# Earlier sums of squares and other unsplit half units in the second SSD layer of a four-layer encoder

## The chip, the cores and the metric

The kernel runs on one core of a Trainium2 chip. The metric is the device time of one execution in microseconds (us). Before the change it is 1605.35 us, the median of three runs (1604.55 to 1608.08). The profile is that of one further execution, which took 1607.9 us.

## The reference

The program is an encoder of four layers over 256 rows of width 1024, all in float32. Each layer is a mixer and an MLP, each behind an RMS norm and with a residual. Layers 0 and 3 have the SSD mixer, which the change is about; layer 1 has a dilated attention and layer 2 a differential attention.

```
def rmsnorm(x, g):
    xf = x.astype(jnp.float32)
    y = xf * lax.rsqrt(jnp.mean(xf * xf, axis=-1, keepdims=True) + RMS_EPS)
    return (y * g.astype(jnp.float32)).astype(x.dtype)
...
def ssd_mixer(h, in_w, conv_w, conv_b, dt_bias, a_log, d_skip, norm_g, out_w):
...
    zxbcdt = h @ in_w
    z, xbc, dt = jnp.split(zxbcdt, [SSD_D_INNER, SSD_D_INNER + SSD_CONV_CH], axis=-1)
...
    xbc = jax.nn.silu(xbc + conv_b)
    xs, bs, cs = jnp.split(xbc, [SSD_D_INNER, SSD_D_INNER + G * N], axis=-1)
...
    y_fwd = ssd_chunk_scan(xs, dt[:, :, 0], a[0], bs, cs)
    y_bwd = flip(ssd_chunk_scan(flip(xs), flip(dt[:, :, 1]), a[1], flip(bs), flip(cs)))
    y = y_fwd + y_bwd + d_skip.astype(jnp.float32).reshape(G, R)[..., None] * xs.astype(jnp.float32)
    y = y.reshape(bsz, s, SSD_D_INNER) * jax.nn.silu(z.astype(jnp.float32))
    y = rmsnorm(y, norm_g).astype(h.dtype)
    return y @ out_w
...
    for i in range(DEPTH):
...
        x = x + h
        x = x + sqrelu_mlp(rmsnorm(x, norm_mlp_g[i]), mlp_w1[i], mlp_w2[i])
    return rmsnorm(x, final_norm_g)
```

The in-projection `h @ in_w` has 6208 columns: 2048 for z, 2048 for x, 1024 for B, 1024 for C and 64 for dt.

## The kernel before, in words

**Layout and arithmetic.** The residual stream lies transposed in SBUF as eight tiles `xT` of 128 features by 256 rows. A float32 matrix product is made from fp32r matmuls: a weight tile is split into `whi` (ScalarE, a cast, line 117) and `wlo` (VectorE, raw minus whi, line 119), the activations likewise into a high and a low tile, and three matmuls (lines 150 to 152) add whi*high, whi*low and wlo*high. A half unit named in `native` skips the split: its raw weights are multiplied with whole float32 activations (line 148), so it needs neither line 117 nor line 119, and its raw buffer stays in use until its matmuls are done.

**Weights.** All weight chunks of a part are listed in the order of use. `pump` (called by `take` and `done`) issues their loads on the SyncE queue (`_dma`, line 105) into five `raw` buffers and their splits into five `whi` and five `wlo` buffers, four chunks ahead of the matmuls in this layer.

**The norm at the start of a layer.** While the MLP before it ends, each of the eight `xT` tiles is finished on VectorE (line 1179), split without its row factor (lines 234 and 235, tiles `spl`), and squared on ScalarE (line 243). GpSimd adds the squares of tiles 1 to 6 to that of tile 0, in the accumulator `sqacc` (line 245); tile 7 keeps its own. `norm_rows` then multiplies both with a constant matrix on TensorE (line 277, four matmul records), which sums over the features and leaves the sum in all partitions; ScalarE adds epsilon (line 279), and seven short VectorE operations (lines 259 to 264) give the reciprocal root `rbc`. `behind`, called on line 277, pins these matmuls behind the TensorE instruction written just ahead of them; later ones aren't held back by it.

**The SSD layer's order.** `ssd_events` lists the work as units with due times, and sorts them. A unit is 256 columns of the in-projection, in two halves of 512 input features; a half has four k tiles and two column tiles, so 24 split matmuls. For layer 3 the order is `CFG["order"]`: z0 z1 B0 x0 C0 x1 B1 x2 z2 C1 x3 C2 B2 z3 x4 and so on. The first two units and the dt unit (64 columns, due at 0.5) work on the unnormalised `spl` tiles and are multiplied by `rbc` when they leave PSUM ("defer"). After unit z0 come the row sums, the evacuation of z0, and `normalised`, which makes the eight tiles `nf` (line 304), `nh` (line 305) and `nl` (line 306) that all later units read; a native half reads `nf`. The dt tile is normalised on VectorE (line 507), transposed on TensorE (line 514, due at 1.5), and run through softplus and logarithm. The dt sums (line 548, due at 4.0) go to DRAM and come back as broadcast rows `bc` (line 579), to which VectorE adds a mask (line 582) and which ScalarE exponentiates (line 607); with `cb` (lines 589 and 591) this gives the factors G (line 620) of the output matmuls (line 632). The x, B and C units leave PSUM through a convolution on VectorE (line 488), and the PSUM banks of units alternate between two.

**The scheduler.** Within each engine the framework orders the instructions when the program is built, by priority (the order in which they are written) among those that its model takes as ready. So the order in a trace need not be that of the source.

Layer 0 has its own settings in `CFG0`, which override those of `CFG`; layer 3 uses `CFG` alone.

Of the kernel before, what the change touches and what calls it, by code (L numbers as in the profile page):

```python
# [51 lines left out]
class Prog:  # L52
# [360 lines left out]
    def ssd_events(self, l, finish):  # L413

        cfg = {**CFG, **(CFG0 if l == 0 else {})}
# [21 lines left out]
        def unit(kind, c0, defer):  # L437

            keys = [(l, kind, c0, i) + (("f32",) if f"{kind}{(c0 - base[kind]) // 256}.{i}" in cfg["native"] else ()) for i in range(2)]

            def fn(c0=c0):
                b = self.bank(f"r{st.setdefault('rot', 0) % 2}")
                st["rot"] += 1
                first = kind == "z" and c0 == 0
                xh, xl = (self.uh, self.ul) if defer else ([st["n"][0][:, k, :] for k in range(KD)], [st["n"][1][:, k, :] for k in range(KD)])
                for i in range(2):
                    wh, wl = self.take(keys[i])
                    for kk in range(4):
                        k = 4 * i + kk
                        for n in range(2):  # L450
                            c = slice(kk * 256 + n * P, kk * 256 + (n + 1) * P)
                            o = b[:, n * T:(n + 1) * T]
                            if wl is None:
                                self.mm3(o, wh[:, c], None, self.nf[:, k, :], None, k == 0 and n == 0, k == 7)
                            else:
                                self.mm3(o, wh[:, c], wl[:, c], xh[k], xl[k], k == 0 and n == 0, k == 7)
                    self.done()
                if first:
                    self.norm_rows("a0")
                evac(kind, c0, b.rearrange("p (n t) -> p n t", n=2), defer)  # L460
                if first:
                    st["n"] = self.normalised(gvec("g_mix", 8 * l, 8))
            plan = [(keys[i], in_w[i * 512:(i + 1) * 512, c0:c0 + 256].rearrange("(k p) f -> p k f", p=P)) for i in range(2)]
            return fn, plan
# [222 lines left out]
        for u, name in enumerate(cfg["order"].split()):  # L687
            kind, i = name[0], int(name[1:])
# [477 lines left out]
    def prepare_part(self, i):  # L1166
# [29 lines left out]
        for _, _, keys, _ in sorted(ev, key=lambda e: e[:2]):  # L1196
# [4 lines left out]

VEC, CST, HEAD = {}, {}, {}
CFG = dict(order='z0 z1 B0 x0 C0 x1 B1 x2 z2 C1 x3 C2 B2 z3 x4 z4 x5 x6 B3 C3 z5 x7 z6 z7',
           native=('B0.0', 'B0.1', 'x0.1', 'x1.1', 'x2.1', 'x3.1', 'x4.1', 'x5.1'),
           sums=4.0, rate=2.4, lag=1.3, tr=1.2, gh0=1.5, gh=0.8, y=2.95, olag=2.0, ogap=4.0, ntail=1, late=10, dt=0.5, defer=2, r2=0.25,
           n_th=1, n_yf=3, n_z2=4, n_bc=2, n_cb=1, n_xt=1, n_e=2, n_G=2, n_t1=1, n_sqt=1, n_ft=3, n_cvx=4, n_cvB=2, n_cvC=2)

CFG0 = dict(order='z0 z1 x0 C0 B0 x1 B1 x2 z2 C1 B2 x3 C2 x4 z3 z4 x5 C3 z5 B3 x6 x7 z6 z7',
            native=('x0.0', 'x0.1', 'B1.0', 'x1.1', 'x2.1', 'x3.1', 'z3.0', 'z4.0'),
            sums=4.75, rate=2.4, lag=1.3, tr=0.8, gh0=0.9, gh=0.4, y=3.2, olag=2.75, ogap=4.0, late=12, r2=0.05, dt=0.5,  # L1210
            n_z2=5, n_e=2, n_G=2, n_cvx=3, n_bc=2, n_cb=1, n_t1=1, n_xt=1, n_th=2, n_yf=1, n_cvB=2, n_cvC=1, n_ft=3)
DIL = dict(bias=2.5, v=5.5, vstep=0.75, s=9.4, sstep=3.7, tr=4.4, hstep=1.3, pv=4.7, out=74.8, ostep=2.2)
# [87 lines left out]
```

## Time and profile before

| what | before |
|---|---|
| median of the runs | 1605.35 us |
| the profiled execution | 1607.9 us |
| its span | 1606.1 us |
| TensorE busy | 1566.8 us (98%) |
| VectorE busy | 1203.5 us (75%) |
| ScalarE busy | 960.3 us (60%) |
| GpSimd busy | 134.1 us (8%) |
| layer 3's SSD mixer | from 1174.6 us to about 1417 us of the span |

PE is TensorE, PEld its weight loads, DVE VectorE, ACT ScalarE, POOL GpSimd, SP SyncE. A line of the timeline gives the start and the duration in us, the engine, the line of the kernel, the operation, what it writes and reads, how many instructions are merged, and in brackets the idle time of the engine before it with what ended it. Matmuls overlap, and their ends are modelled. PEclk is the share of the full TensorE clock that was granted.

### The profile page before, as it was taken

The numbers are of one execution on the slowest core, as the hardware profiler recorded it, in microseconds if no ns is written. First come the engines' busy times: TensorE is split into PE (matmuls) and PEld (weight loads), VectorE is DVE, ScalarE is ACT, GpSimd is POOL, SyncE is SP. The second block draws the span as 40 slices with busy tenths as digits, with TensorE's granted clock in tenths as the row PEclk, the third lists the DMA queues.
The fourth block names the chain that finished last, engine by engine and source line by source line (L and its number), as shares of the span: only waits on it lengthen the run. The fifth ranks groups of instructions, "written<-read, shape, count | busy, mean of one in ns | idle before, by whom it ended". The sixth has DMA issues, their size and how long they took to land.

```text
span 1606.1 us, 32218 instructions
## 1 busy us (share of the span) xinstructions
PE 1566.8 (98%) x12942; PEld 1519.4 (95%) x12942; DVE 1203.5 (75%) x1970; ACT 960.3 (60%) x1620; POOL 134.1 (8%) x120
## 2 busy tenths in 40 slices
PE   9999999999999999999999999999998999999998
PEld 8889899999999999999999999999988988899997
DVE  6999998455697777766556898655588999995554
ACT  6586865444667666655445777444455767664444
POOL 0012121000300000010000101000011122310001
PEclk9999999999999999999999999999999999999999
DMA  7677755676566555546666764666655767656661
GB/s 230 195 223 236 213 188 181 204 223 191 159 200 178 151 170 162 171 148 190 191 196 187 198 193 122 205 192 193 189 163 155 217 210 216 210 173 195 192 193 64
DMA packets 230293, 299.83 MB, mean 187 GB/s; under 512 B 16496, under 2 KB 166256, under 8 KB 230144
## 3 DMA queue, kind: packets, MB, share of 16 engines
q1 hardware_dynamic: 209552, 262.51, 53.4%
q10 hardware_dynamic: 20592, 35.27, 8.0%
q8 instruction: 101, 1.65, 0.4%
q14 instruction: 48, 0.39, 0.1%
HBM read 296.41 MB, written 3.62 MB: 187 GB/s over the span
## 4 chain that ended last, share of the span: by engine, by line
PE 73%; DVE 14%; DMA 5%; ACT 4%; issue 3%; POOL 1%; ACTq 0%; SPq 0%; DVEq 0%; POOLq 0%
PE r L151 12%; PE r L150 12%; PE r L152 12%; PE a L150 8%; PE a L152 8%; PE a L151 8%; DVE wlo L119 3%; DMA raw<-in_ssd_in_w_dram 2%; DMA bc<-scr 2%; PE r L148 2%; DVE cvx L488 1%; PE a L857 1%; PE a L858 1%; PE a L856 1%; DVE bc L582 1%
## 5 line engine op out<-in xcount | busy, mean ns | idle before, releaser
L119 DVE TENSOR_TENSOR wlo<-raw,whi 128x1024 fp32r<-128x1024 f32 (+1 forms) x490 | 592.8, 1217 | 291.4 <-ACT whi L117 287.9
L117 ACT CAST whi<-raw 128x1024 fp32r<-128x1024 f32 (+1 forms) x490 | 503.4, 1034 | 436.3 <-PE r L151 223.6
L151 PE MATMUL r<-spl,whi 128*128 128x256 f32 x1696 | 472.9, 279 | 4.7 <-DVE spl L235 4.7
L150 PE MATMUL r<-spl,whi 128*128 128x256 f32 x1696 | 475.1, 280 | 0.1
L152 PE MATMUL r<-spl,wlo 128*128 128x256 f32 x1696 | 471.4, 278 | 0.4 <-DVE wlo L119 0.4
L151 PEld LDWEIGHTS r<-spl,whi 128*128 128x128 f32 x1696 | 318.4, 188 | 6.5 <-DVE spl L235 6.1
L152 PEld LDWEIGHTS r<-spl,wlo 128*128 128x128 f32 x1696 | 318.6, 188 | 0.7 <-DVE wlo L119 0.6
L150 PEld LDWEIGHTS r<-spl,whi 128*128 128x128 f32 x1696 | 318.2, 188 | 0.6 <-DVE xT L1179 0.3
L150 PE MATMUL a<-hh,whi 128*128 128x256 f32 x944 | 261.4, 277 | 0.0
L151 PE MATMUL a<-hl,whi 128*128 128x256 f32 x944 | 261.3, 277 | 0.0
L152 PE MATMUL a<-hh,wlo 128*128 128x256 f32 x944 | 260.9, 277 | 0.0
L151 PEld LDWEIGHTS a<-hl,whi 128*128 128x128 f32 x944 | 177.6, 188 | 0.0
L150 PEld LDWEIGHTS a<-hh,whi 128*128 128x128 f32 x944 | 177.3, 188 | 0.2 <-ACT whi L117 0.2
L152 PEld LDWEIGHTS a<-hh,wlo 128*128 128x128 f32 x944 | 177.2, 188 | 0.0
L150 PE MATMUL r<-nh,whi 128*128 128x256 f32 x576 | 166.5, 289 | 7.3 <-DVE cvx L488 4.1
L152 PE MATMUL r<-nh,wlo 128*128 128x256 f32 x576 | 163.1, 283 | 1.9 <-DVE wlo L119 1.8
L151 PE MATMUL r<-nl,whi 128*128 128x256 f32 x576 | 162.2, 282 | 0.0
L245 POOL TENSOR_TENSOR sqacc<-sqacc,sq 128x256 f32<-128x256 f32 x48 | 44.5, 927 | 1090.7 <-ACT sq L243 1089.1
L150 PEld LDWEIGHTS r<-nh,whi 128*128 128x128 f32 x576 | 110.4, 192 | 11.8 <-issue 4.2
L152 PEld LDWEIGHTS r<-nh,wlo 128*128 128x128 f32 x576 | 110.1, 191 | 3.2 <-DVE wlo L119 2.3
L151 PEld LDWEIGHTS r<-nl,whi 128*128 128x128 f32 x576 | 109.9, 191 | 0.7 <-issue 0.4
L607 ACT ACTIVATE e<-bc,tb 128x256 f32<-128x256 f32 (+1 forms) x256 | 95.7, 447 | 6.1 <-DVE bc L582 4.8
(246 smaller groups left out, 2521.4 us busy)
## 6 DMA issues: line engine op xcount, KB each, us to landing
raw<-in_mlp_w_dram SPq DMA_DIRECT2D x256, 512.0 KB
raw<-in_ssd_in_w_dram SPq DMA_DIRECT2D x96, 512.0 KB
bc<-scr ACTq DMA_DIRECT2D x32, 768.0 KB
raw<-in_dil_qkv_w_dram SPq DMA_DIRECT2D x48, 512.0 KB
raw<-in_ssd_out_w_dram SPq DMA_DIRECT2D x32, 512.0 KB
raw<-in_dil_qkv_w_dram SPq DMA_DIRECT2D x64, 192.0 KB
raw<-in_diff_qkv_w_dram SPq DMA_DIRECT2D x24, 512.0 KB
raw<-in_dil_out_w_dram SPq DMA_DIRECT2D x8, 512.0 KB
```

The lines of the kernel that those rows point to most:

```text
L117: self.nc.scalar.copy(out=hi[:, :n], in_=raw[:, :n])
L119: self.nc.vector.tensor_tensor(out=lo[:, :n], in0=raw[:, :n], in1=hi[:, :n].bitcast(F32), op=ALU.subtract)
L148: mm(out, lhsT=wh, rhs=xh, start=start, stop=stop, skip_group_check=True)
L150: mm(out, lhsT=wh, rhs=xh, start=start, stop=False, skip_group_check=True)
L151: mm(out, lhsT=wh, rhs=xl, start=False, stop=False, skip_group_check=True)
L152: mm(out, lhsT=wl, rhs=xh, start=False, stop=stop, skip_group_check=True)
L245: nc.gpsimd.tensor_tensor(out=self.sqs[0], in0=self.sqs[0], in1=sq, op=ALU.add)
L488: nc.vector.scalar_tensor_tensor(out=u[:, n, lo:hi], in0=b[:, n, lo + d:hi + d], scalar=col("conv_w", w, cc), in1=u[:, n, lo:hi], op0=ALU. ...
L582: nc.vector.tensor_tensor(out=o, in0=o, in1=mask, op=ALU.add)
L607: X = lambda o, i_, bias: nc.scalar.activation(out=o, in_=i_, func=AF.Exp, bias=bias)
L856: mm(o, lhsT=self.uh[k][:, t], rhs=w_h, start=k == 0, stop=False)
L857: mm(o, lhsT=self.uh[k][:, t], rhs=w_l, start=False, stop=False)
```

## The change

Two edits. In `unit`, the call of `norm_rows` moves into the loop over the two halves and runs after the half that `cfg["rows"]` names: 0 in layer 3, which is after the first half of z0, and 1 in layer 0, which is where it stood. In `CFG`, the native half units change: both halves of B0 become split, and the first half of B1 and the first half of z3 become native. Their number stays eight.

```
                             else:
                                 self.mm3(o, wh[:, c], wl[:, c], xh[k], xl[k], k == 0 and n == 0, k == 7)
                     self.done()
-                if first:
-                    self.norm_rows("a0")
+                    if first and i == cfg["rows"]:
+                        self.norm_rows("a0")
                 evac(kind, c0, b.rearrange("p (n t) -> p n t", n=2), defer)
...
 CFG = dict(order='z0 z1 B0 x0 C0 x1 B1 x2 z2 C1 x3 C2 B2 z3 x4 z4 x5 x6 B3 C3 z5 x7 z6 z7',
-           native=('B0.0', 'B0.1', 'x0.1', 'x1.1', 'x2.1', 'x3.1', 'x4.1', 'x5.1'),
+           native=('B1.0', 'x0.1', 'x1.1', 'x2.1', 'x3.1', 'x4.1', 'x5.1', 'z3.0'), rows=0,
...
-            native=('x0.0', 'x0.1', 'B1.0', 'x1.1', 'x2.1', 'x3.1', 'z3.0', 'z4.0'),
+            native=('x0.0', 'x0.1', 'B1.0', 'x1.1', 'x2.1', 'x3.1', 'z3.0', 'z4.0'), rows=1,
```

## The prediction

> **What bounds the kernel now.** I read the page first (span, chain), then the table of what TensorE waited for in the second SSD layer (1168 to 1412 us of the span), then the busy time by stretch at the places of those waits, then the timelines of the engines around the start of that layer. From the page:
>
> ```profile
> span 1606.1 us, 32218 instructions
> ...
> PE 73%; DVE 14%; DMA 5%; ACT 4%; issue 3%; POOL 1%; ACTq 0%; SPq 0%; DVEq 0%; POOLq 0%
> ```
>
> The chain that ended last runs on TensorE for 73% of the span, so a change pays only where it takes work or waiting off TensorE. The waits of TensorE in this layer, in the columns total us, times, longest:
>
> ```profile
> PE r L632 <- DVE G L620: 2.8, 2, 2.4
> PE r L589 <- ACT xt L601: 2.7, 1, 2.7
> PE r L589 <- DVE cvC L491: 2.4, 1, 2.4
> PE r L150 <- DVE cvx L488: 2.3, 1, 2.3
> PE r L632 <- DVE t L638: 1.9, 1, 1.9
> PE r L514 <- DVE dtT L507: 1.7, 1, 1.7
> PE r L151 <- DVE spl L235: 0.4, 1, 0.4
> ```
>
> These seven rows sum to 14.2 us. Two of them lie where the change works: the 0.4 at the end of unit z0, and the 1.7 in the middle of unit B0, where two transposes of the dt tile wait for VectorE. A wait costs more than itself here, as the busy time by stretch shows (PE busy, then further on PEclk):
>
> ```profile
> core 0: us, PE busy (x) PEld busy (x) DVE busy (x) ACT busy (x) POOL busy (x), PEclk, DMA share, GB/s
> ...
> 1193.83:1197.24 3.41, 1.68 (x9) 1.40 (x9) 3.41 (x10) 1.81 (x6) 0.00 (x0) 1.00 0.53 154
> 1197.24:1200.65 3.41, 3.41 (x11) 2.70 (x9) 3.38 (x7) 1.15 (x2) 0.00 (x0) 0.50 0.41 111
> 1227.96:1231.37 3.41, 0.67 (x6) 0.43 (x5) 1.11 (x1) 3.16 (x9) 1.26 (x1) 1.00 1.03 350
> 1231.37:1234.78 3.41, 1.08 (x3) 0.36 (x3) 3.41 (x8) 0.24 (x1) 0.00 (x0) 0.50 0.78 277
> 1234.78:1238.20 3.42, 3.42 (x17) 3.42 (x18) 3.42 (x10) 2.18 (x6) 0.00 (x0) 0.50 0.10 36
> 1292.81:1296.23 3.42, 1.96 (x17) 1.76 (x15) 0.91 (x2) 3.21 (x7) 0.00 (x0) 1.00 0.50 161
> 1296.23:1299.60 3.37, 2.40 (x20) 1.87 (x21) 3.37 (x4) 3.37 (x8) 1.19 (x1) 1.00 0.00 0
> ```
>
> In the stretch from 1193.83 TensorE was busy 1.68 of 3.41 us, and the next 3.41 us were granted half the clock. In the stretch from 1292.81 it was busy 1.96, and the next kept 1.00. The granted clock is halved for 3.41 us when the stretch before was busy for less than about half; that costs up to 3.41 x 0.5 = 1.71 us of matmul time.
>
> **The change, part by part.** The cuts that follow come from TensorE's timeline (start, duration, engine, line):
>
> ```profile
> 1174.60 0.28 PE L150 MATMUL r<-spl,whi 128*128 128x256 f32 x1
> ...
> 1177.32 0.28 PE L150 MATMUL r<-spl,whi 128*128 128x256 f32 x1
> ...
> 1180.70 0.59 PE L277 MATMUL a<-sqacc,guard 128*128 128x256 f32 x2
> ...
> 1189.87 4.04 PE L148 MATMUL r<-nf,raw 128*128 128x256 f32 x18
> 1195.65 0.33 PE L514 MATMUL r<-head,dtT 64*128 64x64 f32 x2 [1.73 <-DVE dtT L507]
> ...
> 1203.46 3.61 PE L148 MATMUL r<-nf,raw 128*128 128x256 f32 x16
> ```
>
> and from those of GpSimd, ScalarE and VectorE, one after the other:
>
> ```profile
> 1177.84 1.15 POOL L245 TENSOR_TENSOR sqacc<-sqacc,sq 128x256 f32<-128x256 f32 x1 [1.61 <-ACT sq L243]
> ...
> 1182.15 1.05 ACT L117 CAST whi<-raw 128x1024 fp32r<-128x1024 f32 x1 [2.66 <-DMA raw<-in_ssd_in_w_dram]
> 1183.10 0.47 ACT L279 ACTIVATE ms<-a,eps 128x256 f32<-128x256 f32 x1
> ...
> 1179.59 1.21 DVE L119 TENSOR_TENSOR wlo<-raw,whi 128x1024 fp32r<-128x1024 f32 x1
> 1183.23 1.23 DVE L119 TENSOR_TENSOR wlo<-raw,whi 128x1024 fp32r<-128x1024 f32 x1 [2.43 <-ACT whi L117]
> 1184.37 0.29 DVE L259 TENSOR_SCALAR rs_q<-ms 128x256 int32<-128x256 int32 x1
> ...
> 1196.12 0.41 DVE L306 TENSOR_TENSOR nl<-nf,nh 128x256 fp32r<-128x256 f32 x1
> ```
>
> *Sums of squares after the first half of z0.* The layer's first matmul starts at 1174.60, and the 25th, where the second half begins, at 1177.32: a split half is 24 matmuls in 2.72 us. The four guard matmuls of line 277 now stand there instead of at 1180.70. They read the accumulator that GpSimd finishes at 1177.84 + 1.15 = 1178.99. The second half of z0, the dt unit and z1 are issued behind them. The wait is 1178.99 - 1177.32 = 1.67 us, and the 0.4 us that the second half waits today for its last split tile falls into it: net **+1.3**. The lower bound is 0, if the scheduler lets matmuls of the second half ahead of the guard (the `behind` on line 277 only forbids the guard to go earlier). The same four matmuls are issued either way, so nothing is added.
>
> *What that frees.* The guard matmuls need about 1 us from 1178.99, so their sum is there at 1180.0. Today ScalarE reads it only at 1183.10, because it stands in its queue behind a cast that waited 2.66 us for a DMA. At 1180 ScalarE is free, and VectorE has just ended the subtraction of 1179.59 and would have idled 2.43 us until 1183.23. The reciprocal root can start near 1180.8 instead of 1184.37, some 3.5 us earlier, and with it the eight normalised tiles, the last of which is now written at 1196.12 + 0.41. They would end at about 1193, and the dt tile, which is normalised on VectorE after nearly all of them, at about 1192. TensorE ends z1 at 1189.87 today and at about 1191.2 after the +1.3. So the transposes find their tile at or shortly after the time when TensorE wants them: the wait of 1.73 goes, **-1.7** (bounds 0 and -1.73; I take the upper end because both sides move towards each other, by 3.5 and 1.3, against 1.73). With it goes the halved stretch from 1197.24: **-1.7** (0 or -1.71).
>
> *B0 split instead of native.* A native half, 16 matmuls, takes 3.61 us with the end of its last one. A split half ends 0.28 - 0.11 after the start of the next, so 2.89 in the same count. Two halves: 2 x 0.72 = **-1.4**. B0 then needs the pairs nh and nl, tile by tile. They are made from about 1184.5 on and TensorE takes one k in 6 matmuls, 0.68 us, so it follows them closely but not far ahead. The two conversions added cost VectorE 2 x 1.2 us and ScalarE 2 x 1.05 us. VectorE is busy all the time between 1193.83 and 1200.65 (3.41 and 3.38 of 3.41), so they would not be free on top. What covers them is that the conversions ahead of need shift by two chunks: the buffers for whi and wlo stay five, and today's conversions there are for C0 and x1, which TensorE wants 10 us later. If that cover fails, B0 waits for up to 2.4 us. I take 0.
>
> *B1.0 native.* TensorE +0.72, VectorE -1.2, ScalarE -1.05. B1 ends just ahead of the two waits of 2.7 and 2.3 (copies and convolutions that stand behind the loaded rows bc). TensorE arriving there 0.7 later waits 0.7 less: I take 0 (0 to +0.7).
>
> *z3.0 native.* Again +0.72 on TensorE and -1.2 on VectorE, near the 2.4 wait for G. Which of the two is last there changes from one unit to the next; I take 0 (-1.2 to +0.7).
>
> *Sum*: +1.3 - 1.7 - 1.7 - 1.4 = **-3.5 us**, all gained before unit x0 starts. Behind x0 the layer's order of units is unchanged, the loads of bc are issued from a result of TensorE (the dt sums) and so move with it, and the rest of the program follows. The profiled execution took 1607.9 us (span 1606.1 and 1.8 around it); with -3.5 it would take 1604.4. It lies 2.55 above the median of the runs, 1605.35, so against that median the forecast is 1605.35 - 3.5 = **1601.8 us**. A measurement of this kernel tells about 0.2%, 3.2 us, from no change, and the forecast is just past it.
>
> **A rule on the clock.** The row from 1193.83 shows 1.73 us of idling, and the next 3.41 us at 0.50. The Trainium skill ("TensorE: Matmul & The Clock Gate", Why this matters for your kernels) asks for no idle gap of TensorE above about 3 us and has the clock fall after a whole idle window. By that rule neither the old wait of 1.73 nor the new one of 1.67 would touch the clock, and the sum would be -3.5 + 1.7 = -1.8. The trace disagrees: under half a window idle was enough to lose nothing, over half was enough to lose the next.
>
> **Rivals.**
>
> *The clock takes its part back.* The new wait of 1.67 us leaves 3.41 - 1.67 = 1.74 us busy if it lies in one stretch, between the 1.68 that lost the clock and the 1.96 that kept it. Where the stretches lie against the program is chance, so the loss of 1.71 can return at the guard. For it: 1.74 is nearer to 1.68. Against it: it must fall into one stretch. Time: 1601.8 + 1.7 = 1603.5, no change that can be told. The page's rule would give this time too, by leaving the old loss out of the gain.
>
> *The gain stops at the loaded rows.* The dt chain runs on VectorE, interleaved with B0's convolution, and VectorE has been given 2.4 us of conversions and relieved of 1.2 there. If the sums come no earlier, bc lands no earlier, and TensorE, 3.5 us ahead, waits 3.5 us more than 2.7 there. Against it: the 2.43 us hole of VectorE before 1183.23 is used now. Time: 1605.35 to 1606.1 with z3.0's 0.72; 1605.5.
>
> *Later waits shrink as well.* The two waits of 2.7 and 2.3 and the two halved stretches from 1231.37 to 1238.20 are worth 2.7 + 2.3 + 2 x 1.71 = 8.4 us. They come from two bc loads that share the DMA with weights; the raw buffers of B0 are now freed by the conversion and not by its matmuls, so weights come sooner and out of the way, and TensorE comes 0.7 later. If half goes, another -4.2: 1597.6. Against it: nothing in the change shortens the loads themselves.
>
> *Slower: ScalarE behind a late weight load near z4.*
>
> ```profile
> 1293.02 1.05 ACT L117 CAST whi<-raw 128x1024 fp32r<-128x1024 f32 x1 [5.58 <-DMA raw<-in_ssd_in_w_dram]
> ```
>
> ScalarE stood 5.58 us here for a raw tile, with the exponentials for G behind it, and that is the 2.4 us wait of TensorE. Native z3.0 holds one of the five raw buffers until its matmuls end instead of until its conversion. If the following loads are issued later by those 3.61 us, TensorE waits 6.0 instead of 2.4, which leaves two stretches under half busy: 3.6 + 2 x 1.71 + 0.72 = +7.7, less 3.5 is +4.2: 1609.5. It decides when the load of that tile is issued more than about 2 us later against its unit than now. Against it: its own unit comes ten microseconds later, so the cast may be queued later too.
>
> **How the numbers follow.** Forecast, 0.40, with a range of its own from 1600 (no wait at the guard, half of z3.0's 1.2 gained) to 1603.2 (0.7 lost at B1.0 and at z3.0 each), a little over half of it beyond the 0.2% line at 1602.1: 0.23 faster, 0.17 no change. Later waits shrink, 1594 to 1600: 0.27, faster. Clock: 0.15, no change. Gain stops at bc: 0.08, no change. Late load: 0.10, slower. Together faster 0.50, no change 0.40, slower 0.10. Leaving out the slower case and the lower part of the larger gain, 1595.5 to 1606.5 holds 8 in 10.
>
> **What would show it.** Right: the guard matmuls of this layer start within 2 us after the layer's 25th matmul with a wait for GpSimd; the last nl ends 2 to 4 us earlier against the layer's start; no wait on line 514; 0 native matmuls in B0, and the native half of x0 begins about 25.4 us after the layer's first matmul instead of 28.9 (1203.46 - 1174.60). Wrong: a wait on line 152 or 150 for nl or wlo inside B0, a halved stretch right after the guard, or a first bc wait that grows by what the start gained. If x0 comes 3.5 us earlier and the end of the layer doesn't, the step that failed is the one that carries the gain through the layer.

## The result and the profile after

The changed kernel takes **1593.65 us** (median of four runs, 1593.32 to 1596.69) against 1605.61 us for the kernel before in the same comparison: a ratio of 0.993, with a 95% interval from 0.9916 to 0.9943. That is faster by 12 us, more than three times the forecast 3.5 and below the forecast's range of 1600 to 1603.2. A second measurement, reported below, gave 1594.01 us.

The profiled execution took 1596.69 us; its span, from the page:

```profile
span 1594.9 us, 32217 instructions
```

First the second SSD layer as a whole, from its first matmul to the first of the MLP behind it. The busy time by stretch, before:

```profile
1174.60:1416.84 242.24, 227.86 (x1729) 209.52 (x1728) 221.23 (x356) 157.82 (x310) 47.68 (x25) 0.97 0.65 196
```

and after:

```profile
1175.87:1405.95 230.08, 221.38 (x1729) 205.31 (x1727) 221.70 (x356) 158.45 (x310) 53.21 (x25) 1.00 0.66 206
```

The layer is 242.24 - 230.08 = 12.2 us shorter, so all of the gain is in it. The first column behind the length is TensorE's busy time. It idled 14.4 us before and 8.7 after, which gives 5.7. With the same 1729 records it was busy 6.5 us less, and the column PEclk, 0.97 against 1.00, says why: before, 3% of the full clock was not granted on the mean of the layer. So in this pair of profiles half of the gain is waiting, and the other half is clock. A second profile of each kernel (9 and 17 below) gives 11.5 us, 7.4 of them waiting and 4.1 busy time, so the division is not a fixed one.

The waits of TensorE in the layer, after:

```profile
PE r L632 <- DVE t L638: 2.9, 1, 2.9
PE r L589 <- DVE cvC L491: 2.2, 1, 2.2
PE r L150 <- DVE cvx L488: 1.8, 2, 1.5
PE a L277 <- POOL sqacc L245: 1.6, 1, 1.6
PE r L514 <- DVE dtT L507: 0.2, 1, 0.2
```

Five rows and 8.7 us instead of seven and 14.2. The wait at line 514 has all but gone, the guard's is new, and of the pair of 2.7 and 2.3 (cb behind xt, and x2 behind a convolution) nearly nothing is left: the wait of x2 is 0.28 us now, in the fence with line 599 below. The other wait in its row, 1.5 us, lies 195 us into the layer; this profile of before has none there, a second one has 1.34. The wait for G is gone; that for t at the end of the layer grew by 1.0.

**The start of the layer** went as forecast. TensorE's timeline after:

```profile
1175.87 0.28 PE L150 MATMUL r<-spl,whi 128*128 128x256 f32 x1
...
1180.31 0.70 PE L277 MATMUL a<-sqacc,guard 128*128 128x256 f32 x2 [1.56 <-POOL sqacc L245]
...
1193.66 0.33 PE L514 MATMUL r<-head,dtT 64*128 64x64 f32 x2 [0.19 <-DVE dtT L507]
...
1201.30 3.61 PE L148 MATMUL r<-nf,raw 128*128 128x256 f32 x16
```

The guard starts 4.44 us after the layer (6.10 before) behind a wait of 1.56, the transposes wait 0.19 instead of 1.73, and the native half of x0 begins at 1201.30 - 1175.87 = 25.43 us; forecast were 25.4 instead of 28.9. VectorE's last `nl` says the same:

```profile
1194.65 0.42 DVE L306 TENSOR_TENSOR nl<-nf,nh 128x256 fp32r<-128x256 f32 x1
```

It ends 19.2 us after the layer's start; before, 1196.12 + 0.41 - 1174.60 = 21.9.

**Behind x0** the kernels part company. VectorE's timeline in the middle of the layer, before:

```profile
1225.61 1.23 DVE L582 TENSOR_TENSOR bc<-bc,cst 128x1024 f32<-128x1024 f32 x1 [2.85 <-DMA bc<-scr]
1226.75 0.87 DVE L488 SCALAR_TENSOR_TENSOR cvx<-r,vec,cvx 128x255 f32<-128x255 f32 x2
1230.26 1.90 DVE L582 TENSOR_TENSOR bc<-bc,cst 128x1024 f32<-128x1024 f32 x1 [2.64 <-DMA bc<-scr]
1232.09 2.42 DVE L488 SCALAR_TENSOR_TENSOR cvx<-r,vec,cvx 128x255 f32<-128x255 f32 x6
```

and after:

```profile
1220.23 1.23 DVE L582 TENSOR_TENSOR bc<-bc,cst 128x1024 f32<-128x1024 f32 x1 [0.62 <-DMA bc<-scr]
1221.38 0.87 DVE L488 SCALAR_TENSOR_TENSOR cvx<-r,vec,cvx 128x255 f32<-128x255 f32 x2
1223.46 1.23 DVE L582 TENSOR_TENSOR bc<-bc,cst 128x1024 f32<-128x1024 f32 x1 [1.22 <-DMA bc<-scr]
1224.60 2.43 DVE L488 SCALAR_TENSOR_TENSOR cvx<-r,vec,cvx 128x255 f32<-128x255 f32 x6
```

VectorE works in order. It stands at the mask add of line 582 until the rows bc have landed, and six convolution steps of x1 stand behind the second mask add. They read the PSUM bank that unit x2 is to be written into. On TensorE, before:

```profile
1227.83 0.60 PE L599 MATMUL r<-head,cvx 128*128 128x128 f32 x4
1231.17 1.06 PE L589 MATMUL r<-cvC,cvB 128*128 128x256 f32 x2 [2.74 <-ACT xt L601]
1234.57 0.58 PE L150 MATMUL r<-nh,whi 128*128 128x256 f32 x1 [2.33 <-DVE cvx L488]
```

and after:

```profile
1226.20 0.60 PE L599 MATMUL r<-head,cvx 128*128 128x128 f32 x4
1227.08 0.39 PE L150 MATMUL r<-nh,whi 128*128 128x256 f32 x1 [0.28 <-DVE cvx L488]
```

Against the layer's start the second rows landed (the start of the second mask add) at 55.7 before and 47.6 after, 8.1 us earlier, and x2 started at 60.0 and 51.2, 8.8 us earlier. TensorE itself came to the transposes of line 599, ahead of x2, at 53.2 and 50.3, only 2.9 us earlier. So the rows moved further than the engine that they wait for. When ScalarE issued their loads, before:

```profile
1215.86 0.53 ACTq L562 DMA_DIRECT2D scr<-rows  x1
1219.83 0.40 ACTq L579 DMA_DIRECT2D bc<-scr  x1
1220.30 0.45 ACTq L579 DMA_DIRECT2D bc<-scr  x1
```

and after:

```profile
1212.57 0.53 ACTq L562 DMA_DIRECT2D scr<-rows  x1
1214.71 0.40 ACTq L579 DMA_DIRECT2D bc<-scr  x1
1216.66 0.38 ACTq L579 DMA_DIRECT2D bc<-scr  x1
```

The 8.1 us can be read off step by step. The write to scr was issued at 41.3 and 36.7 after the layer's start: 4.6 earlier, of which the dt sums ahead of it make 3.4. Scr took 3.97 us until the first row load and now 2.14: 1.8. The second load was issued 0.47 behind the first and now 1.95: it loses 1.5. It flew 9.96 us and now 6.80: 3.2.

### The profile page after: what moved, and what is told of

It is laid out like the page before. It is cut to its first block, busy times and chain, and to the rows that moved or that the text cites. A ratio compares the mean times of both kernels' runs of the same rounds, so it can differ in the third digit from the quotient of the medians.

```text
span 1594.9 us, 32217 instructions
## 1 busy us (share of the span) xinstructions
PE 1558.7 (98%) x12942; PEld 1513.5 (95%) x12942; DVE 1202.2 (75%) x1970; ACT 961.5 (60%) x1620; POOL 140.6 (9%) x120
## 3 DMA queue, kind: packets, MB, share of 16 engines
q1 hardware_dynamic: 209552, 262.51, 53.2%
## 5 line engine op out<-in xcount | busy, mean ns | idle before, releaser
L150 PEld LDWEIGHTS r<-nh,whi 128*128 128x128 f32 x576 | 109.0, 189 | 12.2 <-DVE cvx L488 5.4
```

The costliest lines, as they stand in the source:

```text
L150: mm(out, lhsT=wh, rhs=xh, start=start, stop=False, skip_group_check=True)
```

## The experiments

All marks below are counted from the layer's first matmul in one profile of each kernel; y0 is the first output matmul of group 0. The layer of the changed kernel came out at 230.1 and 231.3 in two profiles, that of the kernel before at 242.2 and 242.8, so a difference of about a microsecond means nothing. The executions profiled of the kernel before (1607.9 and 1606.99 us) both lay above its medians, so a layer and a median need not differ by the same. Numbers 3 and 6 have the layer of the changed kernel and medians 2.7 and 4.6 above its, so a few microseconds between two medians need not come from the layer. In 5, 6, 10, 15 and 16 each engine runs through the layer in the order of the kernel that was edited, but for what was added to GpSimd; in the others the scheduler moved other instructions too, and their gain or loss is not the edit's alone. Each interval is that of the kernel's own comparison with the kernel before, whose median there lay between 1604.32 and 1605.99.

| kernel | median us | 95% interval of the ratio | second rows landed | y0 | layer |
|---|---|---|---|---|---|
| before | 1605.61 | | 55.6 | 74.1 | 242.2 |
| after | 1593.65 | 0.9916 to 0.9943 | 47.6 | 63.9 | 230.1 |
| 1 row sums alone | 1595.28 | 0.9912 to 0.9954 | 50.7 | 66.3 | 231.3 |
| 2 native halves alone | 1597.11 | 0.993 to 0.9963 | 49.2 | 67.1 | 231.4 |
| 3 after, B1.0 split | 1596.39 | 0.993 to 0.9964 | 50.4 | 67.4 | 230.7 |
| 4 after, z3.0 split | 1597.66 | 0.9937 to 0.9972 | 47.2 | 63.6 | 233.2 |
| 5 before, weights held | 1601.87 | 0.9971 to 0.9989 | 51.5 | 67.6 | 236.1 |
| 6 after, copies (misplaced) | 1598.28 | 0.9943 to 0.9971 | 47.4 | 64.1 | 229.9 |
| 7 before, fillers | 1599.82 | 0.9958 to 0.9982 | 55.0 | 73.8 | 235.6 |
| 8 after, guard later | 1592.27 | 0.9907 to 0.9934 | 47.1 | 63.5 | 228.7 |
| 9 before again | one profile | | 55.2 | 73.9 | 242.8 |
| 10 after, two copies | 1607.96 | 1.0008 to 1.0029 | 59.8 | 77.8 | 245.1 |
| 11 after, fillers | 1600.11 | 0.9955 to 0.9979 | 54.1 | 71.9 | 235.4 |
| 12 before, both held | 1595.76 | 0.993 to 0.9959 | 51.4 | 69.4 | 232.2 |
| 13 before, mask on GpSimd | 1597.13 | 0.9942 to 0.9967 | 55.4 | 71.1 | 234.4 |
| 14 as 8, mask on GpSimd | 1595.96 | 0.9928 to 0.9956 | 46.8 | 63.1 | 232.0 |
| 15 after, one copy | 1602.97 | 0.9973 to 0.9993 | 52.7 | 71.0 | 238.7 |
| 16 after, half a copy | 1598.47 | 0.9944 to 0.997 | 48.5 | 64.9 | 232.4 |
| 17 after again | 1594.01 | 0.9913 to 0.9938 | 47.7 | 64.1 | 231.3 |
| 18 as 8, again | 1593.89 | 0.9907 to 0.9936 | 47.1 | 63.6 | 228.5 |

**1 to 4: which part does it.** Theory A was that native B1.0 keeps weight loads away from the rows, theory B that it takes work off VectorE; the rival, that the earlier start is enough. The four kernels, as changes to the changed kernel:

```
1: native=('B0.0', 'B0.1', 'x0.1', 'x1.1', 'x2.1', 'x3.1', 'x4.1', 'x5.1'), rows=0
2: native as after, rows=1
3: native=('x0.1', 'x1.1', 'x2.1', 'x3.1', 'x4.1', 'x5.1', 'z3.0'), rows=0
4: native=('B1.0', 'x0.1', 'x1.1', 'x2.1', 'x3.1', 'x4.1', 'x5.1'), rows=0
```

> Only the earlier sums of squares; the native half units are those of before. Three theories for the part of the gain that lies behind unit x0 (the two waits near the loaded rows bc and the two halved clock stretches went, some 6 us). Theory A, loads: native B1.0 keeps its raw buffer, so fewer weight loads run beside the rows scr and bc, and these land earlier. Theory B, VectorE: the conversion taken from VectorE at B1.0 (1.2 us) lets the convolution of x1 end sooner. Theory C, start: whatever makes the dt sums some 3 us earlier brings the rest by itself. A and B expect here only the gain at the start, the guard wait of 1.3 against the dt wait and its halved stretch (1.7 + 1.7): about -2, 1603.5 us, with the waits near bc still 4 us or more. C expects -6 or more, 1599 or less.

> Only the new native half units; the sums of squares stay after unit z0. A expects bc to land 5 to 8 us after its issue as with the whole change, and the waits near it mostly gone although the start gains only the 1.4 us of B0 (or loses, if B0 waits for nl): 1597 to 1600 us. B expects the same place to gain 1 to 2 us: 1601 to 1603. C expects the waits near bc to stay: 1603 to 1605.

> The whole change, but B1.0 is split again (seven native halves), which gives 0.7 us of TensorE back. A expects the weight loads to run beside scr and bc again, bc(0,1) to land 3 us or more later against the dt sums, and 3 to 6 us of waiting to return: 1596 to 1599 us. B expects 1.2 us to return at most: 1593 to 1595. C expects 1593 or a little less.

> The whole change, but z3.0 is split again (seven native halves). If the conversion that z3.0 saved is what removed the wait for G near unit z4 (2.4 us before, none after), that wait returns and the time is 1595 to 1597 us; if the earlier start of the layer or the order of the queues removed it, the time is 1592.5 to 1594, 0.7 us less TensorE work included.

Measured: each half of the change alone brings most of the whole, 10 us (1) and 9 us (2); they do not add up, so they remove much the same loss. Number 1 has B1.0 split as before and gains all the same, so the gain does not need native B1.0, contrary to both theories. Numbers 2 and 3 came out at times that theory A gives, but not by its way. In 2 the second load flew 9.6 us, not 5 to 8; its rows landed early because the dt sums came early, at 33.8 us instead of 38.1. In 3 the rows did land 2.8 later than after, and y0 came 3.5 later, but the layer was no longer. What 1, 2 and 3 share is that the dt sums come 2.0 to 4.3 us earlier than before, so the rival stands; 5, 11 and 12 below bear on whether an earlier start is needed. In 1, VectorE's wait at the second mask add is short without any change of native halves:

```profile
1222.33 1.23 DVE L582 TENSOR_TENSOR bc<-bc,cst 128x1024 f32<-128x1024 f32 x1 [1.31 <-DMA bc<-scr]
```

The scheduler also puts cb of group 1 behind x2 after the change, ahead of it before; 1 and 3 have it ahead as before, so that isn't what counts either. Native z3.0 is worth 2 to 3 us late in the layer (4); the wait for G near z4, whose return was one of the two expectations, did not come back, and the median lies above both.

**8 and its repetition: the guard's own wait.** `norm_rows` is called two k tiles later, in the second half of z0:

```
+                        _ = first and (i, kk) == cfg["rows"] and self.norm_rows("a0")
...
-           native=(...), rows=0,
+           native=(...), rows=(1, 1),
```

> The whole change, with the guard matmuls two k tiles later, in the middle of the second half of z0 instead of ahead of it. TensorE waited 1.6 us for GpSimd at the guard; 12 matmuls (1.36 us) whose tiles are there earlier now run in that time, and the sums come no later. If the wait is on the path, the layer is 1.2 to 1.4 us shorter: 1592.3 us. If the loaded rows set the pace of what follows, the same or 0.5 less: 1593 to 1593.7.

Measured: the wait for GpSimd is 0.2 us,

```profile
1176.89 0.70 PE L277 MATMUL a<-sqacc,guard 128*128 128x256 f32 x2 [0.20 <-POOL sqacc L245]
```

and the layer 1.4 us shorter. Run again beside the changed kernel on one chip:

> The changed kernel once more. Its time rests on four runs (1593.32 to 1596.69), and the costs of the extra copies are read against it: the half copy put the second rows off by only 0.9 us and lengthened the layer by 2.3 us, but its median lies 4.8 us above. If 1593.65 is the kernel's own time, the new median is 1593 to 1595 and the half copy costs more outside the layer than in it. If it was a low sample, the new median is 1595 to 1597, and the half copy costs what its layer shows.

> The variant with the row sums two k tiles later once more, beside the changed kernel on the same chip. Its wait at the guard is 0.2 us instead of 1.6 and its layer was 1.4 us shorter. If that carries through, its median is 1 to 2 us below the changed kernel's; if it is lost in later waits, the two agree within 0.7 us.

The changed kernel gave 1594.01 (1593.55 to 1595.48), the variant 1593.89 (1590.75 to 1595.11). They can't be told apart, although the variant's layer is again shorter (228.5 against 231.3). The reference was no low sample.

**9: is the first profile typical?**

> The kernel before, profiled a second time, to see how much of what the first profile shows in the layer is chance. Reading of the first profile: the layer (first matmul of the second SSD layer to the first of the MLP behind it) took 242.2 us, the second load of rows bc flew 9.9 us, x2 started 60.0 us after the layer's start, and two stretches behind it ran at half the clock. If these are the program's own, the second profile gives a layer of 239 to 243 us, a second load of 8.5 us or more, x2 at 58.5 or later. If the layer comes out under 237 us, the first profile was an unlucky one and less than half of the gain behind x0 needs an explanation.

It is: layer 242.8, the second rows 9.6 us in flight, x2 at 59.7, and again three losses of the clock, the third of them this time behind the wait for t, 220 us into the layer.

**5 and 12: the kernel before, with loads kept apart.** In 5 the weight loads of C1.1, x3.0 and x3.1 depend on the second rows (a one-column GpSimd add that writes into raw); TensorE's order is untouched. In 12, besides, the rows (3,1) are issued from GpSimd's queue after the weights of z4.0 have landed; there the order changed in places.

```
-        n = 0
+        n = hold(self, key, raw)
...
+        t = prog.last_rows[:, 0, 0, 0:1]
+        prog.nc.gpsimd.tensor_tensor(out=raw[:, 0:1], in0=t, in1=t, op=ALU.add)
...
+    t = prog.z40[:, 0:1]
+    prog.nc.gpsimd.tensor_tensor(out=bc[:, 0, 0, 0:1], in0=t, in1=t, op=ALU.add)
+    return prog.nc.gpsimd
```

> The kernel before, with three weight loads (C1.1, x3.0, x3.1) held until the second bc load has landed and been masked, by a one-column GpSimd write into their raw buffers; the issue order of TensorE is that of before. In before these three were in flight beside the second bc load, which took 9.9 us (6.8 with the change). Theory A2, that the second bc load's landing sets when x2 can start and that shared DMA made it late: it lands after 6 to 7 us, x2 starts some 3 us earlier against the layer's start, the first of the two halved stretches may stay, and the layer is 3 to 5 us shorter: 1600.5 to 1602.5 us. Rival, that only an earlier dt chain helps and DMA sharing is a bystander: x2 starts as before and the time is 1605 to 1606.

> The kernel before with the weight loads of C1.1, x3.0 and x3.1 held until the second rows have landed (as in the run that held them alone, 1601.9 us), and with the load of the rows (3,1) held until the weights of z4.0 have landed, on GpSimd's queue: in the trace of before that weight load is issued 0.4 us behind these rows, takes 8.4 us, and ScalarE stands 5.6 us at its cast with the exponentials of G behind it. Theory that this second crossing of loads makes the wait for G near z4: ScalarE's wait there falls below 2 us, TensorE waits less than 0.5 us for G, and the time is 1598 to 1600.5. Rival, that the rows then come too late themselves: the wait for G moves to the next output matmuls and the time is 1601.5 or more.

Measured: 5 lands the second rows 4.1 us sooner, 2.5 of it in their flight. Another 1.3 is chance: the wait of 1.63 at the dt transposes fell across two clock stretches (2.38 and 2.82 us busy) and halved none, so the dt sums came earlier. VectorE waits 0.51 us at the mask add,

```profile
1226.11 1.23 DVE L582 TENSOR_TENSOR bc<-bc,cst 128x1024 f32<-128x1024 f32 x1 [0.51 <-DMA bc<-scr]
```

and the layer is 6.1 us shorter in the profile; the medians differ by 2.5, as expected. With 12 it is 10 us in both, more than expected and without an edit at the start of the layer (its dt sums come 1.0 earlier than before). ScalarE's wait for the weights of z4.0 fell from the 5.58 us of before as expected:

```profile
1282.74 1.05 ACT L117 CAST whi<-raw 128x1024 fp32r<-128x1024 f32 x1 [1.28 <-DMA raw<-in_ssd_in_w_dram]
```

TensorE's wait for G should have fallen below 0.5, but was 1.3, against 1.9 in 5. What 12 has over 5 came later: 5 still lost the clock twice, some 180 and 215 us into the layer, and 12 did not; 12 lost it once, 55 us in. So part of the gain comes without an earlier start.

How full the DMA was between the issue of the first rows and the landing of the second, in the busy time by stretch (the last two columns are the busy share and GB/s), before:

```profile
1219.83:1230.26 10.43, 8.60 (x64) 8.07 (x62) 4.81 (x6) 5.64 (x14) 0.44 (x1) 1.00 0.89 237
```

after:

```profile
1214.71:1223.46 8.75, 8.75 (x48) 7.82 (x46) 6.91 (x12) 4.04 (x10) 0.00 (x0) 1.00 0.73 241
```

and in 5:

```profile
1218.15:1226.08 7.93, 7.93 (x58) 7.57 (x58) 4.86 (x6) 3.49 (x8) 0.00 (x0) 1.00 0.70 198
```

Time by rate gives 2.47, 2.11 and 1.57 MB; two rows are 1.57 MB, so 0.9 MB of weights passed between them before, 0.5 after and none in 5. Weights alone do not decide: in 1 it was 1.1 MB (2.64 in all, in 8.90 us), and its rows landed early.

**6, 10, 15 and 16: the changed kernel, with the crowding put back.** Extra copies that nobody reads, in 10 two of 768 KB on GpSimd's queue behind the second row load, in 15 one, in 16 one of 384 KB. In 6, three of weights on ScalarE's queue.

```
+            spare = prog.dr.tile([P, 2, 2, 384], F32, name=f"spare{q}")
+            prog.nc.gpsimd.dma_start(out=spare, in_=src)
```

> The whole change, with 1.5 MB of extra copies within DRAM issued right behind the second bc load (their result is not used); the issue order of TensorE is that of the change. A2: bc lands 3 us or more later, x2 waits for the convolution of x1 by as much, and if a wait passes about half a stretch the clock is halved: the layer is 3 to 7 us longer, 1596.5 to 1601 us. Rival: no change beyond 1 us, 1593 to 1595.

> The changed kernel, with two extra copies of 768 KB each (the same broadcast rows, into DRAM that nobody reads) issued on GpSimd's queue when the rows have landed, beside the first two loads of bc. It adds the traffic that three weight loads put there in the kernel before, and nothing else. Theory that crowded row loads are what held unit x2 up: the second load of bc takes 9 us or more instead of 6.8, x2 starts 3 us or more later than 51.2, TensorE waits there for 3 us or more, and the time is 1596.5 to 1601. Rival, that the layer runs better only because its start and VectorE's chain come earlier: the load may land later, x2 moves by less than 1 us, and the time stays within 1.5 us of the changed kernel's 1593.65.

> The changed kernel with one extra copy of 768 KB beside the row loads instead of two. Two put off the landing of the second rows by 12.2 us and cost 14.3 us; one should put it off by about 6, from 2.8 us ahead of TensorE's first transposes (line 599) to about 3 us behind them. Theory of a margin (rows cost nothing until they land behind those transposes, and then their lateness and a halved clock): layer 233 to 236 us, time 1596.5 to 1600. Rival, that every late microsecond costs in proportion, with no margin: half of 14.3, layer 237.5 us, time 1601.

> The changed kernel with one extra copy of 384 KB beside the row loads, which should put off the landing of the second rows by about 3 us, to about the time of TensorE's first transposes. Theory of a margin: layer 229.5 to 231.5 us, time 1593 to 1595.2. Rival, cost in proportion: a quarter of 14.3, layer 233.8 us, time 1597.2.

Number 6 tells nothing of the question: its copies depended on nothing and ran 2 to 4 us into the span, so the layer is as long as after. In 10 the second rows flew 19.2 us, and the whole gain was gone (1596.5 to 1601 was expected):

```profile
1232.68 1.22 DVE L582 TENSOR_TENSOR bc<-bc,cst 128x1024 f32<-128x1024 f32 x1 [13.64 <-DMA bc<-scr]
1233.82 2.43 DVE L488 SCALAR_TENSOR_TENSOR cvx<-r,vec,cvx 128x255 f32<-128x255 f32 x6
```

```profile
1236.30 0.58 PE L150 MATMUL r<-nh,whi 128*128 128x256 f32 x1 [12.65 <-DVE cvx L488]
```

The first fence is VectorE's timeline, the second TensorE's. The doses: rows later by 0.9, 5.1 and 12.2 us put y0 off by 0.9, 7.1 and 13.9 and the time by 4.8, 9.3 and 14.3. The margin that I had expected isn't there: the changed kernel has 0.28 us of wait at x2 already, and each late microsecond is paid in full, with 1.7 to 2 on top where the wait is long enough to halve the clock. Between 15 and 10, a straight line gives a layer of 241.3 us for rows that land at 55.6 as before, an estimate from these two rows of the table: rows as late as before cost the changed kernel nearly all that it had gained. The half copy cost 4.8 us with only 2.3 in its layer. That stays unexplained, but number 6, with no loss in its layer, lies 4.6 above the changed kernel too.

**7 and 11: matmuls of no use.** In 7, the kernel before gets 16 ahead of the dt transposes and 40 ahead of x2; in 11 the changed kernel gets 32 ahead of x0, so that TensorE comes there as late as before.

```
+        fb = prog.bank("a1")
+        for _ in range(n):
+            prog.behind(prog.nc.tensor.matmul(fb[:, 0:T], lhsT=t[:, 0:P], rhs=t, start=True, stop=True))
```

> The kernel before with 56 added matmuls whose result is not used: 16 (1.8 us) ahead of unit B0, 40 (4.5 us) between the transposes of x0 and unit x2, where TensorE waited 2.7 and 2.3 us. They add only work. If the halved clock comes from idle stretches and costs what the sum says, the halved stretches at B0 and at x2 go: the matmuls of x2 and what follows run at full clock, and the time falls by 2 to 3.5 us in spite of the work, 1602 to 1603.5. If the clock is not set by the idling, the time rises or stays: 1605 to 1608.

> The changed kernel with 32 matmuls of no use (128x128 by 128x256, 0.107 us each, 3.4 us in all) ahead of unit x0, so that TensorE comes to x0 as late as in the kernel before, while the norm, the dt chain of VectorE and the conversions keep their lead. Theory that TensorE's earlier arrival at x0 is what the rest hangs on: the waits at x2 come back, the layer takes 239 us or more, the time is 1601 or more. Rival, that the lead of the dt chain and of VectorE over TensorE is what counts: nothing is lost but the 3.4 us of fillers, or less, where they fill a wait; layer 231 to 233.5 us, time 1594.5 to 1597.

Number 7 has 6 us more matmul work and is faster by 4.5 us, more than expected: y0 comes no earlier than before, but the rest of the layer, 168.1 us before, took 161.8. Its waits at x2 are filled, and no stretch behind them was halved. The 16 ahead of the dt transposes did not do what they were for: the wait there was 1.69 us, and the stretch behind it ran at half the clock. Its sums moved too, half of them ahead of C0, so not all of this is the clock's. Number 11, with its dt sums 0.5 us later than before, landed between both expectations, some 6 us above the changed kernel: 3.4 for the fillers, and the rest because the rows crossed weight loads again (9.3 us in flight) and x2 waited:

```profile
PE r L150 <- DVE cvx L488: 3.6, 2, 2.8
```

**13 and 14: the mask add off VectorE.** The rows land as late as before; only line 582 of group 0 runs elsewhere.

```
-            nc.vector.tensor_tensor(out=o, in0=o, in1=mask, op=ALU.add)
+            (nc.gpsimd if (l, g) == (3, 0) else nc.vector).tensor_tensor(out=o, in0=o, in1=mask, op=ALU.add)
```

> The kernel before, with the mask of the first group's two rows of bc added on GpSimd instead of VectorE (line 582; about 3.7 us each there, worked out from the 1.84 us that GpSimd takes for 128x512 at line 618). The rows land as late as before, beside the same weight loads. Theory that late rows cost time because VectorE stands at the mask add with the convolution of x1 behind it, which holds the PSUM bank that x2 needs: x2 starts 4 us or more earlier than 60.0 after the layer's start, the two waits of TensorE there fall below 2 us together, and the time is 1599 or less. Rival, that the late rows themselves are wanted, by the exponentials, G and the first output matmuls: x2 starts earlier, but the wait moves on to line 632 of group 0, y0 stays later than 72, and the time is 1603 or more.

> The changed kernel with the row sums two k tiles later (1592.27 us), and in addition the first group's masks on GpSimd. Theory of the standing VectorE: what is left of its waits at line 582 (0.6 and 1.2 us after the change) is not on the path any more, because TensorE has no wait at x2; the time is 1591 to 1593. Rival: VectorE is still the one that is late in the middle of the layer, and 2.5 us less work on it bring 1 to 3 us: 1589 to 1591.

On GpSimd each mask add took 2.4 us, not 3.7. In 13, on VectorE:

```profile
1222.88 3.21 DVE L488 SCALAR_TENSOR_TENSOR cvx<-r,vec,cvx 128x255 f32<-128x255 f32 x8
1233.83 1.22 DVE L620 TENSOR_TENSOR G<-e,cb 128x1024 f32<-128x1024 f32 x1 [7.74 <-POOL e L618]
```

and on TensorE:

```profile
1228.43 0.37 PE L150 MATMUL r<-nh,whi 128*128 128x256 f32 x1
...
1238.84 0.58 PE L150 MATMUL r<-nh,whi 128*128 128x256 f32 x1 [3.11 <-DVE cvB L488]
```

The convolution of x1 no longer stands behind the rows, and x2 starts at 53.7 instead of 60.0 without a wait. But VectorE then stands 7.74 us for G, which needs the rows, with B1's convolution behind it, and the unit after x2 waits 3.1. So the late rows act in both ways: y0 comes 3 us earlier, not 10. The time gained 7.4; the part behind y0 isn't explained by this edit, and the scheduler had moved other instructions too. Number 14 shows that nothing of it is left in the changed kernel: other instructions changed places, TensorE waited 5.1 us in one place for a convolution of C, and it came out 2 to 4 us above number 8, outside both expectations.

## Why the prediction was wrong, point by point

*Guard.* Right: +1.3 forecast; the wait measured 1.56 where 1.67 was worked out, and it halved no clock.

*Dt transposes and their halved stretch.* Right: the wait of 1.73 became 0.19, and the stretch behind it ran at full clock.

*B0 split, conversions free of charge.* Right in sum: x0 began at 25.43, and the forecast was 25.4. So -3.5 us up to x0 was right within 0.1.

*B1.0 native, 0.* Right in its size: TensorE's time from the sums to the transposes of line 599 grew by 15.7 - 15.2 = 0.5 us, and putting it back to a split (3) made nothing faster. That the rows landed 2.8 us later in 3 was no part of this term.

*z3.0 native, 0.* Mis-sized: with z3.0 split again (4) the kernel is about 4 us slower, and its layer 2 to 3 us longer, so it was worth more than the 1.2 that was its bound.

*The step that failed* is the last one: "all gained before unit x0 starts. Behind x0 the layer's order of units is unchanged, the loads of bc are issued from a result of TensorE (the dt sums) and so move with it, and the rest of the program follows." The loads did move with the sums, by 3.4 us. But the chain behind the sums is not a fixed length: it lost another 1.1 before scr, 1.8 in scr and net 1.7 in the second row load, and the rows came 8.1 us earlier, TensorE at line 599 only 2.9. Their difference, 5.2 us, is about the sum of the two waits of 2.7 and 2.3. Numbers 10, 15 and 16, which keep the order of all engines, show that the landing carries through to y0 at least one for one; 5 shows that keeping weights away from it is enough for part of the gain; 13 shows VectorE's queue as one of the two ways in which it acts.

*The rival "Later waits shrink as well"* had the right place and nearly the right price: all of its 8.4 us would have given 1601.8 - 8.4 = 1593.4, and 1593.65 was measured. I had counted half of it, with 0.27. That the sum comes so near is in part luck: besides these 8.4, the wait of 2.8 for G and the halved stretch at cvC went, and waits of 1.5 and 1.0 came. Its reason, buffers of B0 that come free earlier, is not the cause: number 1 keeps B0 native and gains. And what I held against it, "nothing in the change shortens the loads themselves", was false: the second row load took 9.96 us before and 6.80 after.

*The clock.* The forecast priced the stretch behind the transposes, and left the others. Before, the waits at x2 and on cvC 189 us into the layer each halved a stretch behind them; the table of busy time shows the second one:

```profile
1361.07:1364.48 3.41, 1.11 (x6) 0.73 (x6) 3.41 (x6) 2.80 (x6) 0.00 (x0) 1.00 0.00 0
1364.48:1367.89 3.41, 3.41 (x17) 1.69 (x16) 3.41 (x4) 3.41 (x10) 2.27 (x1) 0.50 0.34 69
```

After, the wait on cvC is nearly as long (2.2 us) and no stretch of the layer is halved. The stretches follow each other in fixed steps: those halved before begin at 1197.24, 1231.37 and 1364.48, 10 and 39 steps of 3.413 us apart. Counted back in such steps from the halved stretch at 1588.6, the rows after are:

```profile
1346.27:1349.68 3.41, 2.82 (x24) 2.62 (x23) 3.41 (x10) 3.10 (x8) 0.00 (x0) 1.00 0.28 99
1349.68:1353.10 3.42, 1.80 (x12) 1.20 (x14) 3.42 (x4) 3.38 (x8) 0.37 (x1) 1.00 0.00 0
```

So the wait fell across two stretches, and each was busy for more than half. That is chance, and it can turn out otherwise: in the second profile of the changed kernel (17) the wait for t left a stretch only 0.85 us busy, 206 us into the layer, and the next was halved.

*What stays open.* In the changed kernel the way up to y0 hangs on the landing of the rows, and of the gain of 12.2 us 10.2 lie there. The 2.0 us behind y0 are a sum of a removed wait for G, a clock that stayed up and two longer waits at the end; no run separates them. Nor is a late y0 always paid in full: in 7 and 13 the rows land as late as before, and the layer is still 6.7 and 7.8 us shorter, mostly because the part behind y0 took 161.8 and 163.4 us instead of 168.1. So a good part of the loss can be avoided without earlier rows, and which of its later waits and halved stretches follow from the rows is not shown. Nor is it settled how much of the shorter flight is due to fewer weights beside it and how much to the spacing of the two row loads (below).

## What to carry to other kernels

When an edit moves a result that a load hangs on, do not carry the shift through the load: list what flies beside it and how close the loads are issued, before and after, and compare its landing with the engine that will wait for it. A short gain ahead of such a point can be worth more than itself, and a wait of two microseconds can cost another 1.7 by the clock that it lowers. And a wait at a loaded tile on an in-order engine costs what stands behind it in that queue, here a convolution that frees a PSUM bank, not the operation itself.

## What the runs showed of the hardware

*Loads of the same size differ by half in time.* The second row load, 768 KB, took 6.5 to 6.9 us where it was issued about 2 us behind the first (after, 1, 4, 6, 7, 8, 14, 17, 18), 9.3 to 10.0 us where it was issued 0.4 to 0.5 us behind it with weights beside them (before, 2, 3, 9, 11, 13), and 7.2 to 7.5 so close but without weights (5, 12). Part of the difference is the first row load, which is still in flight beside the second: from the issue of the first to the landing of the second the three groups took 8.5 to 8.9, 9.7 to 10.4 and 7.7 to 7.9 us. Number 1 moved more bytes in that time than before, 2.64 MB against 2.47, and was quicker. The spacing was not tried by itself.

*The clock falls after less idling than a whole stretch.* Before, 1.73 us of idling in one stretch halved the next (the prediction's rows), and so did 2.30 us (3.41 - 1.11, in the clock's rows above). The prediction's limit of about half a stretch is a rough one. Over the layer in all profiles, each stretch at full clock in which TensorE was busy for 1.52 us or less was followed by a halved one. Of those from 1.56 to 1.73 some were (1.62 in 13, 1.68 before) and some were not (1.56 after, 1.57 in 5, 1.69 in 11). Above that only one was, with 2.47 us busy, in 2. So what counts is how much of a wait falls into one stretch: the guard's new wait of 1.56 and the 2.21 on cvC after the change halved nothing. The Trainium skill ("TensorE: Matmul & The Clock Gate", Why this matters for your kernels) asks only that no gap be above about 3 us; by that rule the clock's part of this gain, 6.5 us of TensorE's busy time in one pair of profiles and 4.1 in the other, would not exist. The traces disagree.
